# Which engine's queue issues the stores and loads of an SSD step: from SyncE to ScalarE, in a hybrid decoder block

## Chip, core and metric

One core of a Trainium2 chip runs the whole program; all data are fp32. The time is the device time of one execution in microseconds; a kernel's time is the median of several executions.

## The reference

One decoder block over 1024 tokens of 1024 channels, with two mixers side by side and a gated MLP behind them:

```python
u = rmsnorm(h)
gate_a, gate_s, b_a, c_a, v_a, z, xbc, dt_raw = split(u @ w_in)
y_a = (b_a * causal_dwconv3(c_a * v_a)) @ w_a_out
xs, bs, cs = split(silu(causal_dwconv4(xbc) + b))
y = ssd_chunked_scan(xs, softplus(dt_raw + dt_bias), a, bs, cs) + d_skip * xs
y_s = group_rmsnorm(y * silu(z)) @ w_s_out          # 4 groups of 512 channels
h = h + (sigmoid(gate_a) * y_a + sigmoid(gate_s) * y_s) @ w_o
v = rmsnorm(h)
h = h + (silu(causal_dwconv3(v @ w_1) + b) * (v @ w_3)) @ w_down
out = rmsnorm(h)
```

The SSD scan runs over 8 chunks of 128 tokens, for 4 groups of 8 heads (64 channels a head, 128 states a group). Per chunk and group it needs

```python
decay_in = exp(where(causal, a_cum[l] - a_cum[s], -inf))         # per head, 128 x 128
y_diag   = (C B^T * decay_in) @ (dt x)
y_off    = exp(a_cum) * (C @ state)
state    = exp(a_cum[-1]) * state + B^T @ (decay_to_end * dt x)
```

## The kernel before

**Projections.** A projection is done for two blocks of 128 output columns at a time (a pair). By a seven-product scheme over halves of tokens and channels a pair takes seven products, named after their operands (`a11`, `a12`, `s1`, `s2`, `s3`, `a22`, `s4`; their weights `b11`, `b21`, `t1`, `t2`, `t3`, `t4`, `b22`). Each product is 12 matmuls of 128x512 (L255), since each operand is split in a high and a low part. The weights come as two raw tiles of 512 KB a pair (`raw_1`, `raw_2`, loads L158, three buffers), GpSimd forms `t1` to `t4` from them (L292, L293, L304, L310), ScalarE casts the high part (L148, `h_`) and GpSimd or VectorE subtracts for the low one (L149, `l_`).

**SSD steps.** `xBC` goes through the convolution (taps on VectorE, L536), Silu on ScalarE, and is stored to DRAM (`ssd_in<-cv`, L545); `z` too (L561), and the tanh of the gates (L596, `gad`, `gsd`). An SSD step works on one chunk of one group; there are 32 (group by group, 8 chunks each). It loads the decay tile `m` (L630: the negated cumulative log-decay of eight heads, spread over the partitions, 512 KB, two buffers) and `in` (L633: the chunk's x, B, C; two buffers). ScalarE makes the decays (eight Relu with a bias, L639, one Exp, L640). PE transposes x and B (`px`, `pb`) and forms `pc` (L645 to L649); ScalarE copies `pb` to `bk` (L666) and scales `xe` (L658); VectorE makes `xd` (L651), `cb` and `m*cb` (L669). Loads of `eb` (exp of a_cum, two DMAs, L675) and `zt` (the chunk's z, L680, one buffer) follow. PE then does `pd`, `po` and `pst` (L687, L694, L700); VectorE adds `pd` (L702), GpSimd adds `eb` (L704), GpSimd scales the state (`st`, L711), VectorE adds `pst` to it (L715), multiplies by `zt` (L717), and `y` is stored (`yd`, L718). ScalarE squares y (L721), VectorE halves the squares (L722, L724), PE sums them over partitions (`pn`), VectorE and GpSimd make the norm factor `yr` of 128 tokens (L729, L731), and it is stored as 128 single elements (`rd`, L732). All DMAs are issued by SyncE (SP) in queue order: a store that waits for its data holds up what is queued behind it.

**Order of the work.** 8 pairs run first (`BEFORE`), then 29 (`BESIDE`), 203 products. Behind each product `tick()` counts one on, and calls what is due at that count: stage by stage, step `s` is emitted at tick `D0 + DSTEP * s` plus the offset of the stage (`STAGES`: the load of m, of in, decays, transposes, loads of eb and zt, products, squares, norm). The tile scheduler then orders the instructions of each engine by when they can start and by their place in the program, so an engine's order follows the emission only loosely. PSUM holds four buffers `mm` and four `sd`; the `sd` ones serve the products `t1`, `t4`, `b22` and all of the SSD step's, so a late reader of one (`bk` of `pb`, `st` of `pst`) holds up a product. Behind the mixer come sums of `w_down` (`wd`, `td`, many DMAs), `ya`, `so`, the output projection and the MLP; from L816 on these read `gad`, `rd` and `yd`.

Of the kernel before, what the change touches and what calls it, by code (L numbers as in the profile page):

```python
# [11 lines left out]
ALU = mybir.AluOpType  # L12
# [3 lines left out]
P = 128  # L16
# [6 lines left out]
HG = NH // NG  # L23
HD = 64
# [3 lines left out]
NCH = SEQ // P  # L28
# [21 lines left out]
)  # L50


D0, DSTEP = 12, 6
STAGES = LOAD_M, LOAD_IN, DECAY, TRANS, LOAD_Z, DIAG, SQUARES, NORM = -11, -8, -6, -4, -3, 0, 3, 6


AHEAD = 300
# [8 lines left out]
def tile_block(  # L66
# [25 lines left out]
    pe, dve, act, pool, sp = nc.tensor, nc.vector, nc.scalar, nc.gpsimd, nc.sync  # L92
# [38 lines left out]
    def tiny(name, w=1):  # L131
        return scr.tile([P, w], F32, tag="tiny", name=name, bufs=12)
# [30 lines left out]
    nhalf = const([P, 1], "nhalf")  # L163
# [167 lines left out]
    xd_ = [dram.tile([P, 10, SEQ], F32, name=f"ssd_in{g}") for g in range(NG)]  # L331
# [4 lines left out]
    acd = dram.tile([2, P, P], F32, name="acd")  # L336
    yd, rd = {}, {}
# [20 lines left out]
    for t in range(0, NCH, 2):  # L358
        xt = big_tile(f"x{t}", shape=(P, 2, DM))
# [17 lines left out]
    cdb = scm.tile([P, 4, NH, 2], F32, name="cdb")  # L377
# [51 lines left out]
    for j in range(0, 4, 2):  # L429
# [3 lines left out]
        p = Pair(U, w_in[GA + j], w_in[GA + j + 1], f"g{GA + j}", cur["row"])  # L433
        p.first(b4(f"gt{j}"), True)
        head.append(p)
    p = Pair(U, w_in[GA + 4], w_in[GA + 5], f"g{GA + 4}")
# [103 lines left out]
    def conv4(ci, t):  # L540
        cv = b4(f"cv{t}")
        taps(cv, ci, scw[:, t, :], scb[:, t : t + 1])
        act.activation(cv, cv, AF.Silu)
        g, slot = ssd_slot(t)
        sp.dma_start(xd_[g][:, slot, :], cv)  # L545

    def xbc_pair(t):
        cis = [s4(f"xbc{t + i}") for i in range(2)]
# [7 lines left out]
    def z_pair(t):  # L556
        zs = [b4(f"z{t + i}") for i in range(2)]
        pair(U, w_in[ZZ + t], w_in[ZZ + t + 1], f"z{t}", *zs)
        for i, z in enumerate(zs):
            act.activation(z, z, AF.Silu)  # L560
            sp.dma_start(xd_[(t + i) // 4][:, 6 + (t + i) % 4, :], z)  # L561


    taken = {}
# [28 lines left out]
    def gates_done(gts, dst, j):  # L593
        for i, gt in enumerate(gts):
            act.activation(gt, gt, AF.Tanh, scale=0.5)
            sp.dma_start(dst[:, j + i, :], gt)  # L596

    for i, p in enumerate(head):
        if i:
# [9 lines left out]
    def heads(t):  # L609
        return t.rearrange("p (h d) -> p h d", h=HG)  # L610

    def tiles(t):
        return t.rearrange("p (j l) -> p j l", j=4)

    states, stats = {}, {}

    def ssd_chunk(s):

        g, c = divmod(s, NCH)
        nm = f"{g}_{c}"  # L620
        q, cc = c // 2, c % 2
        hsl = slice(g * HG, (g + 1) * HG)
        ts = slice(c * P, (c + 1) * P)
        hts = slice((c % 4) * P, (c % 4 + 1) * P)

        hq = slice(q * NH + g * HG, q * NH + (g + 1) * HG)


        m = ssp.tile([P, HG, P], F32, tag="m", name=f"m{nm}", bufs=2)
        sp.dma_start(m, acd[cc, hq].unsqueeze(0).to_broadcast([P, HG, P]))  # L630
        yield
        inp = ssp.tile([P, 6, P], F32, tag="in", name=f"in{nm}", bufs=2)
        sp.dma_start(inp, xd_[g][:, 0:6, ts])  # L633
        xt, bt, ct = inp[:, 0:4, :], inp[:, 4, :], inp[:, 5, :]
# [37 lines left out]
        eb = c2(f"eb{nm}")  # L672
        if c > 0:
            for i in range(2):
                sp.dma_start(  # L675
                    tiles(eb)[i * HD : (i + 1) * HD],
                    ead[cc, hq.start + i : hq.stop : 2].unsqueeze(0).to_broadcast([HD, 4, P]),
                )
        zt = ssp.tile([P, 4, P], F32, tag="z", name=f"zt{nm}", bufs=1)
        sp.dma_start(zt, xd_[g][:, 6:10, ts])  # L680
        yield

        st = states.get(g)
        pd = sd_tile(f"pd{nm}")
        for h in range(HG):
            i, j = h % 2, h // 2
# [11 lines left out]
        if c < NCH - 1:  # L698
            pst = sd_tile(f"pst{nm}")
            pe.matmul(pst, bk, xe, start=True, stop=True)  # L700
        dve.tensor_tensor(xt, xt, tiles(pd), op=ALU.add)
        if st is not None:  # L702
            dve.tensor_tensor(eb, po, eb, op=ALU.mult)
            pool.tensor_tensor(xt, xt, tiles(eb), op=ALU.add)  # L704
        if c < NCH - 1:
            if st is None:
                st = ssp.tile([P, HALF], F32, tag="st", name=f"st{g}", bufs=1)
                act.copy(st, pst)
                states[g] = st
            else:  # L710
                pool.tensor_tensor(  # L711
                    heads(st), heads(st),
                    cdb[:, q, hsl, cc : cc + 1].to_broadcast([P, HG, HD]), op=ALU.mult,
                )
                dve.tensor_tensor(st, st, pst, op=ALU.add)  # L715

        dve.tensor_tensor(xt, xt, zt, op=ALU.mult)  # L717
        sp.dma_start(yd[g, c // 4][:, :, hts], xt)  # L718
        yield
        sq = eb  # L720
        act.activation(sq, xt.rearrange("p j l -> p (j l)"), AF.Square)  # L721
        dve.tensor_tensor(sq[:, : 2 * P], sq[:, : 2 * P], sq[:, 2 * P :], op=ALU.add)  # L722
        sums = ssp.tile([P, P], F32, tag="ss", name=f"ss{nm}", bufs=1)
        dve.tensor_tensor(sums, sq[:, :P], sq[:, P : 2 * P], op=ALU.add)  # L724
# [2 lines left out]
        pe.matmul(pn, sums, ones[:, :1], start=True, stop=True)  # L727
        rs = tiny(f"yss{nm}")
        dve.tensor_scalar(rs, pn, 1.0 / HALF, EPS, op0=ALU.mult, op1=ALU.add)  # L729
        r = tiny(f"yr{nm}")  # L730
        pool.tensor_tensor(r, rs, nhalf, op=ALU.pow)  # L731
        sp.dma_start(rd[g, c // 4][hts].unsqueeze(1), r)  # L732
        yield

    def at(n, f):
# [3 lines left out]
    for s in range(NS):  # L739
        d = D0 + DSTEP * s  # L740
        ch = ssd_chunk(s)
        for o in STAGES:
            at(d + o, lambda ch=ch: next(ch))
# [253 lines left out]
    for i in range(NFF):  # L997
# [5 lines left out]
        cv = b4(f"fcv{i}")  # L1003
# [221 lines left out]
```

## Time and profile before

| what | value |
| --- | --- |
| median of 3 runs | 2109.27 us (2107.75 to 2114.36) |
| the profiled execution's own time | 2107.57 us |
| its span in the trace | 2105.9 us |
| its mean granted clock of PE | 0.967 |
| busy in the span: PE, DVE, POOL, ACT | 1956.1, 1365.6, 1306.4, 904.3 us |
| stretch 0 to 285: PE busy, clock, DMA share | 262.00 us of 285, 0.96, 0.36 |
| stretch 285 to 1081, with 30 of the 32 SSD steps | 697.02 us of 796, 0.94, 0.58 |
| stretch 1081 to 1200 | 115.25 us of 119, 1.00, 0.92 |
| stretch 1200 to 2105 | 881.81 us of 905, 0.99, 0.47 |

Names are those of the program without buffer numbers. In a row "A <- B: 10.5, 6, 2.9" the instruction A waited for B, 10.5 us in 6 waits, the longest 2.9. A row of a timeline gives start, duration (us), engine, line, operation, `out<-in`, and in square brackets the idle time ahead and who ended it. SPq and ACTq are the sequencers of SP and ACT, which issue DMAs; PEld is PE's loading of weights. "DMA share" is the mean busy share of the 16 DMA engines.

### The profile page before, as it was taken

Reading aid. Unit: us, or ns where it says so; the run is one execution under the profiler, and the core shown is the slowest. Engines: PE = TensorE matmul, PEld = TensorE weight load, DVE = VectorE, ACT = ScalarE, POOL = GpSimd, SP = SyncE. Lnnn points to the kernel's source line nnn. Section 1 sums busy time; section 2 is a strip of 40 time slices with the busy share of each in tenths; the row PEclk is TensorE's granted clock in tenths of the full one; section 3 lists DMA queues with packets and bytes.
Section 4 is the critical chain, followed back from the end, with each engine's and each line's share of the span. In section 5 each row is a group of like instructions: output and inputs, shape, how many; then the busy total and the mean of one; then the engine's idle time right before and its main releaser. Section 6 shows DMA issues by size and latency. Waiting matters only on the chain.

```text
span 2105.9 us, 26136 instructions
## 1 busy us (share of the span) xinstructions
PE 1956.1 (93%) x8978; PEld 1594.3 (76%) x8978; DVE 1365.6 (65%) x1588; ACT 904.3 (43%) x1687; POOL 1306.4 (62%) x959
## 2 busy tenths in 40 slices
PE   6899998997998989897899999997999999999998
PEld 5788877776776777675677888886788888887887
DVE  8756986755676557664567562438776677784555
ACT  5354455444744553533333332444433333343444
POOL 7777785674666567566744432347888778853552
PEclk9899998999999999999899999998999999999999
DMA  4243235545445743667999674442322234468664
GB/s 145 72 157 105 110 131 139 147 119 137 146 119 111 158 142 97 128 165 212 249 282 389 244 248 159 159 161 97 120 105 103 98 130 155 146 210 285 198 200 150
DMA packets 184724, 338.47 MB, mean 161 GB/s; under 512 B 19856, under 2 KB 92304, under 8 KB 183568
## 3 DMA queue, kind: packets, MB, share of 16 engines
q1 hardware_dynamic: 184592, 336.80, 52.0%
q8 instruction: 71, 1.16, 0.3%
q14 instruction: 61, 0.50, 0.1%
HBM read 247.34 MB, written 89.41 MB: 160 GB/s over the span
## 4 chain that ended last, share of the span: by engine, by line
PE 41%; DMA 9%; DVE 2%; POOL 1%; issue 1%; ACT 0%; SPq 0%; POOLq 0%; ACTq 0%; DVEq 0%
PE so L255 7%; DMA td<-wd 3%; PE d L1018 3%; PE d L1020 3%; PE d L1019 3%; PE pt4up L255 3%; PE pb22up L255 3%; PE pt3up L255 3%; PE pt2up L255 3%; PE pb11up L255 3%; PE pt1up L255 3%; PE pb21up L255 3%; PE ya L255 2%; DMA wd<-in_w_down 2%; PE wo L891 1%; PE wo L892 1%
## 5 line engine op out<-in xcount | busy, mean ns | idle before, releaser
L639 ACT ACTIVATE m<-m,tk 128x128 f32<-128x128 f32 x256 | 78.8, 389 | 196.7 <-DMA m<-acd 182.6
L536 DVE SCALAR_TENSOR_TENSOR cv<-xbc,scw,cv 128x1024 f32<-128x1024 f32 x72 | 128.2, 1803 | 18.1 <-ACT cv L532 18.1
L536 DVE SCALAR_TENSOR_TENSOR fcv<-fci,fcw,fcv 128x1024 f32<-128x1024 f32 x44 | 77.8, 1768 | 27.9 <-ACT fcv L532 27.9
L149 POOL TENSOR_TENSOR l_ws<-raw_ws,h_ws 128x512 fp32r<-128x512 f32 x32 | 45.8, 1433 | 78.9 <-issue 29.0
L722 DVE TENSOR_TENSOR eb<-eb 128x256 f32<-128x256 f32 x32 | 21.3, 666 | 83.7 <-ACT eb L721 83.3
L148 ACT CAST h_ws<-raw_ws 128x512 fp32r<-128x512 f32 x64 | 38.5, 621 | 81.5 <-PE so L255 54.7
L255 PE MATMUL so<-yh,h_ws 128*128 128x512 f32 x256 | 69.6, 393 | 1.5 <-ACT h_ws L148 0.7
L658 ACT ACTIVATE xe<-px,tk 128x64 f32<-128x64 f32 x256 | 55.9, 329 | 31.0 <-DVE xd L651 30.9
L255 PE MATMUL so<-yl,h_ws 128*128 128x512 f32 x256 | 68.8, 389 | 0.0
L255 PE MATMUL so<-yh,l_ws 128*128 128x512 f32 x256 | 68.7, 390 | 0.0
L149 DVE TENSOR_TENSOR l_ws<-raw_ws,h_ws 128x512 fp32r<-128x512 f32 x32 | 29.0, 910 | 59.2 <-PE so L255 34.3
L149 POOL TENSOR_TENSOR l_wo<-raw_wo,h_wo 128x512 fp32r<-128x512 f32 x24 | 33.3, 1390 | 52.1 <-ACT h_wo L148 25.0
L292 POOL TENSOR_TENSOR t1up<-raw_2up,raw_1up 128x512 f32<-128x512 f32 x22 | 34.6, 1572 | 46.3 <-DMA raw_2up<-in_w_up 41.8
L715 DVE TENSOR_TENSOR st<-st,pst 128x512 f32<-128x512 f32 x24 | 16.5, 687 | 70.7 <-POOL st L711 63.3
L255 PEld LDWEIGHTS so<-yh,h_ws 128*128 128x128 f32 x256 | 47.4, 188 | 12.8 <-ACT h_ws L148 2.3
L717 DVE TENSOR_TENSOR in<-in,zt 128x512 f32<-128x512 f32 x32 | 44.4, 1388 | 18.7 <-POOL in L704 18.1
L255 PEld LDWEIGHTS so<-yh,l_ws 128*128 128x128 f32 x256 | 48.0, 188 | 10.5 <-DVE l_ws L149 0.5
L255 PEld LDWEIGHTS so<-yl,h_ws 128*128 128x128 f32 x256 | 48.1, 188 | 10.1
L148 ACT CAST h_wo<-raw_wo 128x512 fp32r<-128x512 f32 x48 | 29.7, 622 | 56.7 <-PE wo L892 26.8
L891 PE MATMUL wo<-l_wo,mh 128*128 128x512 f32 x128 | 50.9, 398 | 3.2 <-DVE l_wo L149 3.2
L1006 DVE TENSOR_TENSOR fcv<-fcv,h 128x1024 f32<-128x1024 f32 x22 | 38.9, 1767 | 22.6 <-ACT fcv L1005 22.6
L149 POOL TENSOR_TENSOR l_wa<-raw_wa,h_wa 128x512 fp32r<-128x512 f32 x16 | 27.8, 1743 | 39.3 <-PE ya L255 16.7
(1060 smaller groups left out, 6734.5 us busy)
## 6 DMA issues: line engine op xcount, KB each, us to landing
m<-acd SPq DMA_DIRECT2D x32, 512.0 KB, 5.6
raw_ws<-in_w_s_out SPq DMA_DIRECT2D x32, 512.0 KB, 4.2
ssd_in<-cv SPq DMA_DIRECT2D x24, 512.0 KB, 2.7
in<-ssd_in SPq DMA_DIRECT2D x32, 384.0 KB, 3.8
raw_wo<-in_w_o SPq DMA_DIRECT2D x24, 512.0 KB, 3.4
wd<-in_w_down SPq DMA_DIRECT2D x22, 512.0 KB, 6.2
td<-wd SPq DMA_DIRECT2D x44, 256.0 KB, 5.9
raw_1up<-in_w_up SPq DMA_DIRECT2D x22, 512.0 KB, 3.4
```

The lines of the kernel that those rows point to most:

```text
L148: act.copy(hi, v)
L149: (eng or pool).tensor_tensor(lo, v, f32(hi), op=ALU.subtract)
L255: pe.matmul(ps, wt[:, k, :], ct[:, k, :], start=(start and n == 0), stop=(stop and n == 11),)
L536: dve.scalar_tensor_tensor(cv, ci[:, j : j + SEQ], w[:, j : j + 1], cv, op0=ALU.mult, op1=ALU.add)
L639: act.activation(m[:, h, :], m[:, h, :], AF.Relu, bias=a)
L658: act.activation(xe[:, hc], px[:, hc], AF.Copy, scale=tk[:, 2, cc, q, g * HG + h : g * HG + h + 1],)
L717: dve.tensor_tensor(xt, xt, zt, op=ALU.mult)
L891: pe.matmul(pss[t], mh, wl, start=False, stop=False)
L1006: dve.tensor_tensor(cv, cv, h3, op=ALU.mult)
L1018: pe.matmul(ps, aa[0][:, ts], bb[0], start=k == 0, stop=False)
L1019: pe.matmul(ps, aa[0][:, ts], bb[1], start=False, stop=False)
L1020: pe.matmul(ps, aa[1][:, ts], bb[0], start=False, stop=k == KF - 1)
```

## The change

- ScalarE issues, in place of SyncE: the stores of cv, z, the gates and y, and the loads of m, eb (two) and zt. SyncE keeps the loads of weights and of `in`, and the stores of `tad` and `rd`.
- D0 goes from 12 to 11, LOAD_M from −11 to −9: all stages are emitted one tick earlier, the load of m one later, at tick 2 + 6s, where the squares of step s − 2 are emitted just ahead of it.
- The store of y stands behind the square of the same tile.
- The scaling of the state by its decay (GpSimd) is emitted ahead of the addition of `pd`.
- The norm factors of four chunks are gathered in a tile of 128x4 and stored once: 8 stores of 512 elements in place of 32 of 128.

```diff
--- before.py
+++ after.py
@@ -50,8 +50,8 @@
 )
 
 
-D0, DSTEP = 12, 6
-STAGES = LOAD_M, LOAD_IN, DECAY, TRANS, LOAD_Z, DIAG, SQUARES, NORM = -11, -8, -6, -4, -3, 0, 3, 6
+D0, DSTEP = 11, 6
+STAGES = LOAD_M, LOAD_IN, DECAY, TRANS, LOAD_Z, DIAG, SQUARES, NORM = -9, -8, -6, -4, -3, 0, 3, 6
 
 
 AHEAD = 300
@@ -542,7 +542,7 @@
         taps(cv, ci, scw[:, t, :], scb[:, t : t + 1])
         act.activation(cv, cv, AF.Silu)
         g, slot = ssd_slot(t)
-        sp.dma_start(xd_[g][:, slot, :], cv)
+        act.dma_start(xd_[g][:, slot, :], cv)
 
     def xbc_pair(t):
         cis = [s4(f"xbc{t + i}") for i in range(2)]
@@ -558,7 +558,7 @@
         pair(U, w_in[ZZ + t], w_in[ZZ + t + 1], f"z{t}", *zs)
         for i, z in enumerate(zs):
             act.activation(z, z, AF.Silu)
-            sp.dma_start(xd_[(t + i) // 4][:, 6 + (t + i) % 4, :], z)
+            act.dma_start(xd_[(t + i) // 4][:, 6 + (t + i) % 4, :], z)
 
 
     taken = {}
@@ -593,7 +593,7 @@
     def gates_done(gts, dst, j):
         for i, gt in enumerate(gts):
             act.activation(gt, gt, AF.Tanh, scale=0.5)
-            sp.dma_start(dst[:, j + i, :], gt)
+            act.dma_start(dst[:, j + i, :], gt)
 
     for i, p in enumerate(head):
         if i:
@@ -627,7 +627,7 @@
 
 
         m = ssp.tile([P, HG, P], F32, tag="m", name=f"m{nm}", bufs=2)
-        sp.dma_start(m, acd[cc, hq].unsqueeze(0).to_broadcast([P, HG, P]))
+        act.dma_start(m, acd[cc, hq].unsqueeze(0).to_broadcast([P, HG, P]))
         yield
         inp = ssp.tile([P, 6, P], F32, tag="in", name=f"in{nm}", bufs=2)
         sp.dma_start(inp, xd_[g][:, 0:6, ts])
@@ -672,12 +672,12 @@
         eb = c2(f"eb{nm}")
         if c > 0:
             for i in range(2):
-                sp.dma_start(
+                act.dma_start(
                     tiles(eb)[i * HD : (i + 1) * HD],
                     ead[cc, hq.start + i : hq.stop : 2].unsqueeze(0).to_broadcast([HD, 4, P]),
                 )
         zt = ssp.tile([P, 4, P], F32, tag="z", name=f"zt{nm}", bufs=1)
-        sp.dma_start(zt, xd_[g][:, 6:10, ts])
+        act.dma_start(zt, xd_[g][:, 6:10, ts])
         yield
 
         st = states.get(g)
@@ -698,6 +698,11 @@
         if c < NCH - 1:
             pst = sd_tile(f"pst{nm}")
             pe.matmul(pst, bk, xe, start=True, stop=True)
+        if st is not None and c < NCH - 1:
+            pool.tensor_tensor(
+                heads(st), heads(st),
+                cdb[:, q, hsl, cc : cc + 1].to_broadcast([P, HG, HD]), op=ALU.mult,
+            )
         dve.tensor_tensor(xt, xt, tiles(pd), op=ALU.add)
         if st is not None:
             dve.tensor_tensor(eb, po, eb, op=ALU.mult)
@@ -708,17 +713,13 @@
                 act.copy(st, pst)
                 states[g] = st
             else:
-                pool.tensor_tensor(
-                    heads(st), heads(st),
-                    cdb[:, q, hsl, cc : cc + 1].to_broadcast([P, HG, HD]), op=ALU.mult,
-                )
                 dve.tensor_tensor(st, st, pst, op=ALU.add)
 
         dve.tensor_tensor(xt, xt, zt, op=ALU.mult)
-        sp.dma_start(yd[g, c // 4][:, :, hts], xt)
         yield
         sq = eb
         act.activation(sq, xt.rearrange("p j l -> p (j l)"), AF.Square)
+        act.dma_start(yd[g, c // 4][:, :, hts], xt)
         dve.tensor_tensor(sq[:, : 2 * P], sq[:, : 2 * P], sq[:, 2 * P :], op=ALU.add)
         sums = ssp.tile([P, P], F32, tag="ss", name=f"ss{nm}", bufs=1)
         dve.tensor_tensor(sums, sq[:, :P], sq[:, P : 2 * P], op=ALU.add)
@@ -727,9 +728,12 @@
         pe.matmul(pn, sums, ones[:, :1], start=True, stop=True)
         rs = tiny(f"yss{nm}")
         dve.tensor_scalar(rs, pn, 1.0 / HALF, EPS, op0=ALU.mult, op1=ALU.add)
-        r = tiny(f"yr{nm}")
-        pool.tensor_tensor(r, rs, nhalf, op=ALU.pow)
-        sp.dma_start(rd[g, c // 4][hts].unsqueeze(1), r)
+        if c % 4 == 0:
+            stats[g, c // 4] = tiny(f"yr{nm}", 4)
+        r = stats[g, c // 4]
+        pool.tensor_tensor(r[:, c % 4 : c % 4 + 1], rs, nhalf, op=ALU.pow)
+        if c % 4 == 3:
+            sp.dma_start(rd[g, c // 4].rearrange("(c p) -> p c", c=4), r)
         yield
 
     def at(n, f):
```

In the changed kernel the lines behind the edit move: L702 is the state's scaling, L706 the addition of `pd`, L709 that of `eb`, L716 `st`, L718 the product with `zt`, L721 the square, L722 the store of y, L734 `yr`, L736 the store of `rd`.

How the instructions stand on three engines, before and after. First ScalarE around the decays of one step, the seventh of the second group (`m1_6`; `h_` are casts of weights, `eb1_4` the square of the step two before, `bk1_5` the copy of the transposed B); before:

```order
L148 CAST h_t4cv3_5256<-t2cv3_5181 128x512
L148 CAST h_b22cv3_5313<-raw_2cv3_5178 128x512
L639 ACTIVATE m1_6_5130<-m1_6_5130,tk_225 128x128 x5
L282 COPY m1cv3_5132<-pb11cv3_5113 128x512
L639 ACTIVATE m1_6_5130<-m1_6_5130,tk_225 128x128 x3
L148 CAST h_b21ba2_5386<-raw_1ba2_5338 128x512
L721 ACTIVATE eb1_4_4996<-in1_4_4818 128x512
L640 ACTIVATE m1_6_5130<-m1_6_5130 128x1024
L666 COPY bk1_5_5172<-pb1_5_5156 128x128
```

The same place on ScalarE in the changed kernel:

```order
L148 CAST h_t4cv3_5275<-t2cv3_5172 128x512
L630 DMA m1_6_5166<-acd_92 128x1024
L639 ACTIVATE m1_6_5166<-m1_6_5166,tk_225 128x128 x8
L148 CAST h_b22cv3_5293<-raw_2cv3_5169 128x512
L640 ACTIVATE m1_6_5166<-m1_6_5166 128x1024
L721 ACTIVATE eb1_4_4960<-in1_4_4781 128x512
L722 DMA yd11_99<-in1_4_4781 512x1x128
L680 DMA zt1_5_5164<-ssd_in1_85 128x4x128
L666 COPY bk1_5_5132<-pb1_5_5116 128x128
```

The load of m has come to stand directly ahead of the activations that read it, and ahead of the square of step s − 2, though it is emitted behind it; the store of y and the load of zt stand between the square and `bk`.

Now SyncE's queue around the first steps of the second group (`raw_` are weight loads, `rd01_96` and `yd10_97` stores of norm factors and of y); before:

```order
L158 DMA raw_2z10_4698<-in_w_in 128x1024
L732 DMA rd01_96<-yr0_7_4248 128x1
L630 DMA m1_2_4297<-acd_92 128x1024
L545 DMA ssd_in2_86<-cv9_4147 128x1024
L718 DMA yd10_97<-in1_0_3996 512x1x128
L680 DMA zt1_1_4372<-ssd_in1_85 128x4x128
L675 DMA eb1_1_4369<-ead_109 64x4x128 x2
L561 DMA ssd_in2_86<-z8_4154 128x1024
L633 DMA in1_2_4402<-ssd_in1_85 128x6x128
L158 DMA raw_1cv2_4846<-in_w_in 128x1024
```

The same place on SyncE in the changed kernel:

```order
L633 DMA in1_1_4171<-ssd_in1_85 128x6x128
L158 DMA raw_1z10_4607<-in_w_in 128x1024
L736 DMA rd01_96<-yr0_4_3604 128x4x1
L158 DMA raw_2z10_4682<-in_w_in 128x1024
L633 DMA in1_2_4362<-ssd_in1_85 128x6x128
L158 DMA raw_1cv2_4867<-in_w_in 128x1024
```

Of ten transfers the loads of weights and of `in` are left, and one store of norm factors for four chunks.

Last, GpSimd around the scaling of the state (`st1`) in the fifth step of the second group; before:

```order
L304 TENSOR_TENSOR t3ba2_5456<-raw_2ba2_5412 128x512
L731 TENSOR_TENSOR yr1_3_5068<-yss1_3_5066,nhalf_80 128x1
L711 TENSOR_TENSOR st1_4263<-st1_4263,cdb_226 128x512
L704 TENSOR_TENSOR in1_4_4818<-in1_4_4818,eb1_4_4996 128x512
L149 TENSOR_TENSOR l_b11ba2_5342<-raw_1ba2_5338,h_b11ba2_5341 128x512
```

The same place on GpSimd in the changed kernel:

```order
L734 TENSOR_TENSOR yr1_0_4415<-yss1_3_5031,nhalf_80 128x1
L304 TENSOR_TENSOR t3ba2_5473<-raw_2ba2_5395 128x512
L702 TENSOR_TENSOR st1_4234<-st1_4234,cdb_226 128x512
L709 TENSOR_TENSOR in1_4_4781<-in1_4_4781,eb1_4_4960 128x512
L149 TENSOR_TENSOR l_b11ba2_5346<-raw_1ba2_5342,h_b11ba2_5345 128x512
```

The scaling of the state stays behind `t3`, which needs the pair's second weight tile, and ahead of the addition of `eb`.

## The prediction

> **What bounds the kernel now.** I read the page first, then the busy times by stretch, then the waits of TensorE and of the others in the stretch where it idles, and last the timelines around its longest waits.
>
> ```profile
> span 2105.9 us, 26136 instructions
> ```
>
> The first number of a stretch is its length; then come the busy times of PE, PE's weight loads, DVE, ACT and POOL, the granted clock, the DMA share and GB/s.
>
> ```profile
> 285.00:1081.00 796.00, 697.02 (x3421) 556.81 (x3422) 511.18 (x651) 375.83 (x882) 506.89 (x393) 0.94 0.58 153
> ...
> 1100.00:1150.00 50.00, 47.04 (x206) 37.86 (x204) 32.86 (x40) 17.14 (x25) 21.88 (x14) 1.00 1.00 360
> 1200.00:1300.00 100.00, 100.00 (x439) 82.13 (x438) 49.74 (x58) 31.66 (x48) 29.05 (x21) 1.00 0.55 184
> ```
>
> From 1200 PE is full, and the change alters no instruction there. What can move lies in the 796 us from 285 to 1081, where 30 of the 32 SSD steps run beside the projections: PE idles 796 − 697 = 99 us there, and at a granted clock of 0.94 its work takes about 48 us (796 × 0.06) more than at full clock. No other engine is near its limit (DVE 511, POOL 507, ACT 376 of 796), nor the DMA (0.58). So it is order and lateness: which waits of PE end last?
>
> ```profile
> PE pc L649 <- DVE st L715: 10.5, 6, 2.9
> ...
> PE pt1xb L255 <- ACT bk L666: 9.8, 1, 9.8
> ...
> PE pb22ba L255 <- DVE ba L312: 6.1, 1, 6.1
> ...
> PE pt1z L255 <- ACT bk L666: 5.9, 1, 5.9
> ...
> PE pb22z L255 <- ACT bk L666: 5.2, 1, 5.2
> ...
> PE pb22cv L255 <- ACT bk L666: 4.3, 1, 4.3
> ...
> PE pt4xb L255 <- ACT bk L666: 3.6, 1, 3.6
> PE pt1cv L255 <- DVE st L715: 3.5, 2, 3.0
> PE pt1g L255 <- DVE st L715: 3.0, 1, 3.0
> PE pt1ba L255 <- DVE st L715: 2.7, 1, 2.7
> ```
>
> (Total us, times, longest.) Two families: PSUM held by `bk` on ACT (28.8 us) and by `st` on DVE (19.7 us). Behind each stands a wait of another engine:
>
> ```profile
> ACT m L639 <- DMA m<-acd: 182.6, 26, 16.4
> ...
> DVE st L715 <- POOL st L711: 63.3, 17, 8.3
> ```
>
> ACT's decay activations (L639) stand ahead of `bk` and of the casts of weights, and wait for the load of the decay tile `m`. DVE's `st` waits for POOL's. That load stands in SP's queue, among stores that wait for results:
>
> ```profile
> SPq L718 <- DVE in L717: 105.4, 27, 8.2
> ...
> SPq L732 <- POOL yr L731: 97.5, 26, 9.7
> ```
>
> One case in full: SP, then ACT, then PE.
>
> ```profile
> 832.55 0.33 SPq L732 DMA_DIRECT2D rd<-yr  x1
> 832.97 1.42 SPq L630 DMA_DIRECT2D m<-acd  x1
> ```
> ```profile
> 844.91 0.40 ACT L639 ACTIVATE m<-m,tk 128x128 f32<-128x128 f32 x1 [10.94 <-DMA m<-acd]
> ```
> ```profile
> 849.30 1.22 PE L255 MATMUL pb22ba<-us4h,h_b22ba 128*128 128x512 f32 x2 [6.06 <-DVE ba L312]
> ```
>
> The store of `r` (512 bytes in 128 writes of one element) goes out 0.42 us ahead of the load, and the load reaches ACT 11.9 us after its issue. The moved bytes from 826 to 846, in slices of 0.5 us, show why:
>
> ```profile
> GB/s 0 0 0 0 0 0 0 0 0 229 229 401 189 0 34 0 0 0 0 0 0 0 57 8 25 33 0 16 8 25 8 8 16 123 336 348 349 345 271 120
> ```
>
> For about 9 us everything slumps behind the small writes, then the 512 KB come at 340 GB/s. Where a weight load stands ahead instead:
>
> ```profile
> 883.42 0.38 SPq L630 DMA_DIRECT2D m<-acd  x1
> ```
> ```profile
> 887.62 0.99 ACT L639 ACTIVATE m<-m,tk 128x128 f32<-128x128 f32 x3 [3.59 <-DMA m<-acd]
> ```
>
> There it takes 4.2 us, and PE runs on without a gap. The first and the last pair of that kind are issued at
>
> ```profile
> 323.87 0.37 SPq L630 DMA_DIRECT2D m<-acd  x1
> ...
> 1014.52 0.48 SPq L630 DMA_DIRECT2D m<-acd  x1
> ```
>
> and I count eight in all among the 30 steps: 8.1 to 13.1 us each from issue to use, the others mostly 4.2 to 6.4.
>
> **The change part by part.** *Loads of `m`, on ACT's queue, behind the squares.* No `r` store can stand ahead of it on ACT's queue, and no store that waits on SP. The bk family (28.8) and the 6.1 (the case above) go: **−35 us**. Next late is ACT itself: the load is now issued only once ACT reaches it, directly ahead of the eight L639 that need it. What excuses this is that ACT's sequencer runs ahead of its engine:
>
> ```profile
> L721 ACTq EVENT_SEMAPHORE  x2: 17/28/38, 591.6 to 591.7; - x2
> L721 ACT ACTIVATE eb<-in x1: 630/630/630, 599.1 to 599.1; 128x512 f32<-128x512 f32 x1
> ```
>
> The sequencer dealt with the square at 591.7, the engine came to it at 599.1. So a load may go out while earlier casts still run.
>
> *SP without the stores of y, cv, z and gates.* SP keeps weight loads, `in`, `tad` and the new `r` store. Its wait for `in` of DVE (105 us) goes, most of L732's as well, so the second weight tile of a pair comes on time. That matters for `st`:
>
> ```profile
> 396.05 1.28 POOL L292 TENSOR_TENSOR t1ba<-raw_2ba,raw_1ba 128x512 f32<-128x512 f32 x1 [7.49 <-DMA raw_2ba<-in_w_in]
> ...
> 401.77 1.05 POOL L711 TENSOR_TENSOR st<-st,cdb 128x512 f32<-128x512 f32 x1
> ```
>
> POOL waited 7.5 us for a weight tile, and its scaling of `st` came 5.7 us behind. The scaling's earlier place in the source hardly moves it on POOL, so this part depends on SP alone, and I take two thirds of 19.7: **−13 us**.
>
> Idle falls by 48 of 99 us. The low clock comes with the idling (0.94 here, 1.00 where PE is full), so I let it go in proportion: 48 × 48/99 = **−23 us**. Gross −71.
>
> *Costs: ACT's issues.*
>
> ```profile
> L675 SPq DMA_DIRECT2D eb<-ead x56: 579/607/3518, 316.2 to 1057.7; - x56
> ```
> ```profile
> L680 SPq DMA_DIRECT2D zt<-ssd_in x32: 379/622/5712, 193.6 to 1048.2; - x32
> ```
> ```profile
> L718 SPq DMA_DIRECT2D yd<-in x32: 550/552/618, 304.5 to 1077.7; - x32
> ```
>
> 56 × 0.61 + 32 × 0.62 + 32 × 0.55 + 30 × 0.38 for `m` (883.42) + about 32 stores of cv, z and gates at the same 0.38 = 34 + 20 + 18 + 11 + 12 = 95 us, 3.1 us a step, on a queue that is busy 376 of 796 us. Hidden while the sequencer is ahead: 0. Unhidden everywhere: 95. I take an eighth, **+12 us**, nearer the hidden end because ACT's engine sits idle over half the stretch. The y store moved behind the square finds its data ready, as the square reads the same tile: 0; on SP it would have waited. A load of `zt` or `eb` that has to wait for its buffer now holds ACT's casts, and PE behind them; that is in the 12.
>
> *The `r` stores: 8 of 512 elements in place of 32 of 128.*
>
> ```profile
> rd<-yr SPq DMA_DIRECT2D x31, 0.5 KB, 9.1
> ```
>
> The trace has no store of 4 elements per partition. Bounds: 9 us of slump if rows go side by side, as the store of `ced` (128 pieces of 8 bytes) suggests; 36 if the count of elements decides.
>
> ```profile
> 91.28 0.38 SPq L508 DMA_DIRECT2D ced<-ce  x1
> ```
> ```profile
> GB/s 164 164 238 229 303 426 426 139 123 140 134 134 3 106 25 0 25 25 82 16 188 352 252 111 113 16 0 0 0 0 0 0 90 401 410 148 82 123 344 164
> ```
>
> (86 to 106 in slices of 0.5 us.) Behind it the rate is low for under 4 us. I take 12 us for a new one, nearest the `rd` row. 24 slumps less is in the 71 already; a slump hits all queues, `m` on ACT's too, in 8 steps of 32: 8 × 1.25 = **+10 us** (0 to 8 × 17).
>
> *Given back.* 1100 to 1150 runs at a DMA share of 1.00 with the sums of `w_down`; a PE that gets there 71 us sooner doesn't shorten those transfers. Bounds: 0 (SP is freer, they start sooner too) and 71 (they end as before). I take **+8 us**, near the low end, since PE idles only 3 us in that stretch although it is full.
>
> The stages one tick earlier (D0) and `m` one tick later: a tick is one product, 796 us over 203, 4 us; the last step ends 4 us sooner, with PE's own products still to do: 0. The later `m` has two ticks less, 8 us, ahead of its use; it is paid for in the 12 above.
>
> Sum: −35 − 13 − 23 + 12 + 10 + 8 = −41. The profiled execution took 2107.6 us (span 2105.9); 2107.6 − 41 = 2066.6. The median of the runs before is 2109.3, 1.7 above it: **2068 us**. A difference of 0.3% (6 us), the spread of the three runs, is what can be told from none.
>
> **The rivals.** *ACT becomes the late queue (slower).* A load directly ahead of its user on an in-order engine exposes its latency: issue 0.4 plus 5 us, 30 times. For it: ACT's casts feed every product of PE, and the squares now ahead wait for DVE. Against it: the sequencer's lead of 7 us above. Each microsecond per step that PE feels costs 30 × 1.48 (the clock included) = 44 us. The gain left is 71 − 18 = 53, with the other two costs off, so from 1.2 us per step on it is slower; at 2 us, 2107.6 − 53 + 89 = **2144 us**. Chance 0.10. At 0.8 us it gives 2090: 0.08.
>
> *The `r` store scales with its elements (slower).* A slump of 36 us is more than weight tiles cover. An estimate of that cover: three raw tiles, of which each feeds three or four products of 4 us, some 20 us with the split ones. 8 × (36 − 20) = 128 us of idle: 2107.6 − 71 + 20 + 128 = **2185 us**. It turns from gain to loss at a slump of 26 us (8 × 6.4 = 51). For it: one element per write is the same size as before. Against it: `ced`. Chance 0.06. The Trainium skill ("DMA: Bandwidth & Descriptors", Specifications) says that a transfer under 512 B makes the DMA engine read, modify and write; by that the same 4096 small writes would cost the same in all, which speaks for this rival; the two slumps above agree that such writes are dear, not on how they add up.
>
> *The queue doesn't matter (no change).* The transfers share one set of engines, which the slump at 835 shows to hit everything; if that, not SP's order, makes `m` late, the moves give nothing, and the eight long stores cost what 24 short ones saved: **2109 us**. Against it: 883.42, 4.2 us beside 11.9. Chance 0.10. The Trainium skill ("Trainium Kernel Development and Optimization", Key Constraints) states that transfers issued from SP, ACT and POOL run on the same 16 engines and that several issuers only save issue time. The trace shows what it leaves out: on one queue the issuer also waits for stores' data, 105 and 97 us here.
>
> *Every late step recovers.* Idle falls to 25 us (a quarter), −74, clock −36, costs +12 for ACT alone: 2107.6 − 98 = **2010 us** or less. For it: the remaining 44 us of small waits may be the same cascade. Chance 0.10.
>
> **How the numbers follow.** My forecast, 2068 with its own range of 2025 (costs at their hidden ends, 2037, and the small waits with them) to 2100 (costs doubled, 2098), has 0.56. Faster: 0.56 + 0.08 + 0.10 = 0.74; same 0.10; slower 0.10 + 0.06 = 0.16. The range for 8 in 10 leaves out the long slump (0.06), most of ACT's (0.08) and half of the big recovery (0.05): 2008 to 2115.
>
> **What would show it.** Right: ACT's wait for `m` with no single one above 8 us; PE's waits behind `bk` and `st` gone; idle from 285 to 1081 near 50 us and the clock near 0.97; SP waiting for weight buffers, not for `in` of DVE or `yr`. Wrong: eight gaps of 10 us or more in PE behind the new `r` stores; ACT's `m` wait still at 180 us with PE's casts behind it (the first rival); or an unchanged PE idle with only the names of the waits changed.

## The result and the profile after

| | before | changed |
| --- | --- | --- |
| median | 2111.08 us (2107.75 to 2114.36, 4 runs) | 2039.18 us (2035.02 to 2042.32, 4 runs) |
| ratio | | 0.9658, 95% interval 0.9633 to 0.9683 |
| profiled execution: own time, span | 2107.57, 2105.9 us | 2035.02, 2033.3 us |
| its mean granted clock | 0.967 | 0.981 |

The change makes the kernel 3.4% faster, more than the forecast of 2068 and inside its range. From one profiled execution to the other it is 72.6 us.

The stage of the SSD steps ends where PE starts on `ya`: at 1080.77 us before, at 1005.50 after. The busy times of the changed kernel from 285 us to that end, its columns as in the prediction:

```profile
285.00:1005.50 720.50, 673.40 (x3414) 540.01 (x3412) 526.76 (x646) 377.77 (x878) 512.14 (x389) 0.97 0.55 166
```

The same stretch of the kernel before, to its own end:

```profile
285.00:1080.77 795.77, 696.79 (x3420) 556.58 (x3421) 510.95 (x651) 375.83 (x882) 506.66 (x393) 0.94 0.58 153
```

The stage is 75.3 us shorter. PE's idle time in it falls from 99.0 to 47.1 us (−51.9), and the same matmuls take 23.4 us less at a clock of 0.97 in place of 0.94. Behind the stage 2.7 us are given back. The busy times of the other engines change little (the most is DVE's, 511 to 527 us).

PE's waits in the changed kernel, in that stretch (total us, times, longest):

```profile
PE pst L700 <- DVE yss L730: 13.1, 6, 3.1
PE pc L649 <- DVE st L716: 11.7, 8, 5.5
PE pt1ba L255 <- DVE st L716: 4.7, 1, 4.7
PE po L694 <- DVE gt L314: 3.0, 1, 3.0
...
PE pt4g L255 <- ACT bk L666: 1.1, 1, 1.1
...
PE pt1z L255 <- DVE st L716: 0.5, 1, 0.5
```

The family behind `bk` is gone but for 1.1 us, and so is the wait for `ba`. The family behind `st` is not: 16.9 us of 19.7 are still there. What these engines wait for:

```profile
ACT m L639 <- DMA m<-acd: 94.3, 22, 9.4
DVE st L716 <- POOL st L702: 68.7, 18, 11.6
```

ACT's wait for `m` is half of what it was (182.6), its longest 9.4 in place of 16.4. DVE's wait for GpSimd's scaling of the state has not become shorter (63.3 before). SyncE's queue in the changed kernel:

```profile
SPq L633 <- DMA yd<-in: 229.8, 27, 18.9
SPq L158 <- DVE yss L730: 53.4, 10, 9.9
...
SPq L736 <- POOL yr L734: 24.2, 7, 7.4
```

It no longer waits for results of y, cv, z and the gates, but the waiting has not gone: the load of `in` (L633) needs a buffer that is free only once the store of y has landed, and the weight loads stand behind that. This wait was there before the change too, at less than half:

```profile
SPq L633 <- DMA yd<-in: 97.6, 22, 9.3
```

### The profile page after: what moved, and what is told of

It reads as the page before. It is cut to its first block, busy times and chain, and to the rows that moved or that the text cites. A ratio compares the mean times of both kernels' runs of the same rounds, so it can differ in the third digit from the quotient of the medians.

```text
span 2033.3 us, 25995 instructions
## 1 busy us (share of the span) xinstructions
PE 1933.0 (95%) x8978; PEld 1578.5 (78%) x8978; DVE 1390.5 (68%) x1588; ACT 909.9 (45%) x1687; POOL 1309.6 (64%) x959
## 3 DMA queue, kind: packets, MB, share of 16 engines
q10 hardware_dynamic: 61696, 70.27, 11.6%
## 4 chain that ended last, share of the span: by engine, by line
PE 63%; DMA 13%; DVE 9%; POOL 7%; issue 5%; ACT 3%; SPq 0%; ACTq 0%; POOLq 0%; DVEq 0%
PE so L255 7%; PE pt2up L255 3%; PE pt4up L255 3%; DMA wd<-in_w_down 3%; PE pt3up L255 3%; PE pb22up L255 3%; PE pb11up L255 3%; PE pt1up L255 3%; PE pb21up L255 3%; PE d L1022 2%; PE d L1024 2%; PE d L1023 2%; PE ya L255 2%; PE pb22xb L255 1%; PE pt4xb L255 1%
## 5 line engine op out<-in xcount | busy, mean ns | idle before, releaser
L149 POOL TENSOR_TENSOR l_wo<-raw_wo,h_wo 128x512 fp32r<-128x512 f32 x24 | 34.3, 1432 | 50.8 <-ACT h_wo L148 24.9
L716 DVE TENSOR_TENSOR st<-st,pst 128x512 f32<-128x512 f32 x24 | 16.5, 686 | 71.0 <-POOL st L702 68.7
L718 DVE TENSOR_TENSOR in<-in,zt 128x512 f32<-128x512 f32 x32 | 44.9, 1404 | 18.8 <-POOL in L709 16.4
L669 DVE TENSOR_TENSOR m<-m,cb 128x1024 f32<-128x1024 f32 x32 | 53.2, 1662 | 0.4
L896 PE MATMUL wo<-h_wo,ml 128*128 128x512 f32 x128 | 50.8, 398 | 0.0
```

The lines of the kernel that those rows point to most:

```text
L149: (eng or pool).tensor_tensor(lo, v, f32(hi), op=ALU.subtract)
L669: dve.tensor_tensor(m, m, cb.unsqueeze(1).to_broadcast([P, HG, P]), op=ALU.mult)
L896: pe.matmul(pss[t], ml, wh, start=False, stop=k == NK - 1)
```

## The experiments

The kernel before took 2111, 2100, 2100 and 2099 us in the four sets of runs (the result and the three sets below), so kernels are compared by their ratio to the kernel before in the same set. In the table each is the kernel before or the changed kernel with the difference named; m, r, and so on are the loads and stores of these tiles.

| run | kernel | ratio | 95% interval | stage, us | PE idle in it, us | ACT's wait for m | st's for GpSimd |
| --- | --- | --- | --- | --- | --- | --- | --- |
| | before | 1 | | 795.8 | 99.0 | 182.6 | 63.3 |
| e1_gather_only | before, r gathered | 0.9725 | 0.9698 to 0.9753 | 734.7 | 58.0 | 146.8 | 46.5 |
| e2_m_on_act | before, m on ScalarE | 0.9806 | 0.9783 to 0.9828 | 750.1 | 66.0 | 119.0 | 67.0 |
| f1_gather_m_act | before, both | 0.9621 | 0.9606 to 0.9637 | 712.0 | 44.8 | 98.4 | 55.1 |
| g2_row_m_act | before, m on ScalarE, r as rows | 0.9567 | 0.9544 to 0.9591 | 698.5 | 35.0 | 68.8 | 24.9 |
| | changed | 0.9658 | 0.9633 to 0.9683 | 720.5 | 47.1 | 94.3 | 68.7 |
| g1_changed_again | changed, once more | 0.9675 | 0.9654 to 0.9696 | 724.7 | 45.9 | 99.9 | 64.7 |
| e3_no_gather | changed, r in 32 stores | 0.9857 | 0.9834 to 0.988 | 751.6 | 72.5 | 103.2 | 83.7 |
| e4_m_on_sp | changed, m on SyncE | 0.9715 | 0.9688 to 0.9742 | 728.6 | 50.6 | 126.3 | 58.7 |
| f2_row_store | changed, r as rows | 0.962 | 0.9599 to 0.9641 | 710.1 | 35.3 | 83.8 | 24.3 |
| f3_in_later | changed, in emitted later | 0.9673 | 0.9656 to 0.969 | 711.5 | 41.5 | 91.2 | 64.6 |
| f4_eb_doubled | changed, eb in 4 pieces | 0.9712 | 0.9695 to 0.9729 | 722.3 | 46.6 | 89.5 | 67.6 |
| g3_eb_zt_on_sp | changed, eb and zt on SyncE | 0.9696 | 0.9678 to 0.9713 | 726.9 | 51.7 | 110.7 | 69.6 |
| g4_stores_on_sp | changed, y, cv, z, gates on SyncE | 0.9693 | 0.9668 to 0.9719 | 720.6 | 44.7 | 97.6 | 72.7 |

The stage runs from 285 us to the first `ya` in each profiled execution; the idle time is its length less PE's busy time. The profiled executions lie anywhere in a kernel's spread of about 0.3%, so a few us between two stages tell nothing; the ratios decide.

### First four: which of the two suspects makes m late

My theory was that both count, the small writes of the norm factors and SyncE's queue. One rival had the small writes alone, the other the queue alone.

**e1_gather_only.** Edit to the kernel before:

```diff
-        r = tiny(f"yr{nm}")
-        pool.tensor_tensor(r, rs, nhalf, op=ALU.pow)
-        sp.dma_start(rd[g, c // 4][hts].unsqueeze(1), r)
+        if c % 4 == 0:
+            stats[g, c // 4] = tiny(f"yr{nm}", 4)
+        r = stats[g, c // 4]
+        pool.tensor_tensor(r[:, c % 4 : c % 4 + 1], rs, nhalf, op=ALU.pow)
+        if c % 4 == 3:
+            sp.dma_start(rd[g, c // 4].rearrange("(c p) -> p c", c=4), r)
```

> The kernel before with one edit: the norm factors of four chunks are gathered and stored once (8 stores of 512 elements on SyncE). If small writes ahead of the load of m make it late, and both the queue and their number count (my theory), most of the eight long loads go: 25 to 40 us faster, ACT's wait for m from 183 to about 130 us. If the small writes alone are the cause (rival), the whole gain is here: 60 to 75 us faster. If only SyncE's waiting stores are the cause (second rival): within 6 us of the kernel before, the eight long loads still there behind other stores.

0.9725, so 56 us (2044.1 beside 2099.9): between what my theory and the rival gave. The edit has a second effect that I had not named: 24 stores fewer stand in SyncE's queue, and SyncE's waits for `yr` fall from 97.5 to 20.5 us. So this run alone doesn't tell small writes from queue; f1_gather_m_act and g2_row_m_act do, further down. PE's longest waits of this kernel:

```profile
PE pt1xb L255 <- ACT bk L666: 10.1, 1, 10.1
PE pb22z L255 <- ACT bk L666: 9.6, 1, 9.6
```

Two of the old gaps are still there, and ACT still waits 146.8 us for `m`. Ahead of both gaps one of the eight stores that are left goes out 0.47 us before the load of `m`; the pairs are

```profile
480.58 0.37 SPq L735 DMA_DIRECT2D rd<-yr  x1
481.05 0.44 SPq L630 DMA_DIRECT2D m<-acd  x1
```
```profile
660.38 0.37 SPq L735 DMA_DIRECT2D rd<-yr  x1
660.85 0.50 SPq L630 DMA_DIRECT2D m<-acd  x1
```

and ACT gets to work on `m` at 492.60 and 674.68, 11.6 and 13.8 us after the issue. This is the case of the prediction again. For y and cv SyncE waits longer than before (105.4 and 52.7):

```profile
SPq L718 <- DVE in L717: 159.7, 27, 12.8
SPq L545 <- ACT cv L543: 63.3, 9, 12.3
```

**e2_m_on_act.** Edit to the kernel before:

```diff
-        sp.dma_start(m, acd[cc, hq].unsqueeze(0).to_broadcast([P, HG, P]))
+        act.dma_start(m, acd[cc, hq].unsqueeze(0).to_broadcast([P, HG, P]))
```

> The kernel before with one edit: the load of m is issued by ScalarE, at its old tick. My theory: it gets past SyncE's stores, but the 32 slumps behind the norm factors still hit it: 20 to 35 us faster, the waits behind bk mostly gone. Small writes alone: within 6 us. ScalarE as the late queue: slower, with ACT's wait for m at 183 us or more and PE's waits behind casts longer.

0.9806, 41 us faster, a little past what I gave. The rival in which ScalarE becomes the late queue falls: ACT's wait for `m` went down to 119.0 with the load directly on its own queue, and so did PE's waits behind `bk`:

```profile
PE pb22cv L255 <- ACT bk L666: 2.5, 1, 2.5
PE pt4xb L255 <- ACT bk L666: 1.5, 1, 1.5
```

The rival of the small writes alone (no more than 6 us) falls too.

**e3_no_gather.** Edit to the changed kernel: the lines of e1_gather_only the other way round.

> The changed kernel without the gathering: 32 stores of 128 single elements again, all else as changed. My theory: 24 more slumps of 9 us, each felt by loads on every queue: 15 to 30 us slower than the changed kernel (2054 to 2069). Small writes alone: 2095 or more. Queue alone: within 6 us of 2039.

0.9857 beside 0.9658: 42 us slower than the changed kernel, more than my theory gave (15 to 30), less than the rival's. Without the gathering the changed kernel is even slower than e2_m_on_act, in which `m` alone moved (0.9834 to 0.988 beside 0.9783 to 0.9828). So something in the other edits costs, some 11 us. As in e1_gather_only, SyncE's waits for `yr` change with the stores (24.2 to 132.4 us), so this run doesn't show the 42 us to be the small writes alone.

**e4_m_on_sp.** Edit to the changed kernel: `act.dma_start(m, ...)` back to `sp.dma_start(m, ...)`.

> The changed kernel with the load of m back on SyncE, at its new tick, all else as changed. My theory: SyncE no longer waits for y, cv, z or gates, but for the buffer of in (230 us in the changed kernel), so m comes late behind that: 10 to 25 us slower than 2039. If it is the small writes alone: within 6 us. If the issue on ScalarE costs: up to 10 us faster.

0.9715, 8 to 12 us slower than the changed kernel (0.9675 and 0.9658), at or below the low end of what I gave, and its interval overlaps with the second measurement's; a wait of 5.0 us behind `bk` is back. That this is less than the 41 us of e2_m_on_act because the stores have left SyncE is not shown: e1_gather_only, with all stores still there, is as fast (0.9725).

### Next four: what the two edits are worth together, and the costs

**f1_gather_m_act.** Edit to the kernel before: those of e1_gather_only and e2_m_on_act, and nothing else.

> The kernel before with two edits only: the gathered store of norm factors, and the load of m on ScalarE at its old tick. Theory after the first four runs (these two carry the gain, each alone 0.9725 and 0.9806 of the time before, and the stores, eb, zt, the early state and the ticks carry nothing): within 0.4% of the changed kernel's 0.966. If the moved stores carry a part of their own (rival): 0.971 or above. If the other issues on ScalarE cost what I put on them (12 us): 0.960.

0.9621. These two edits are worth the whole change, and its interval (0.9606 to 0.9637) touches the changed kernel's first one (0.9633 to 0.9683) and lies below its second (0.9654 to 0.9696). They are partly the same gain: alone they take 2.75% and 1.94%, together 3.79%. And the stores of y, cv and z are left on SyncE, with their waits:

```profile
SPq L718 <- DVE in L717: 159.7, 29, 14.0
SPq L545 <- ACT cv L543: 47.1, 7, 12.2
```

Nearly 160 us of waits for y, with weight loads behind, make this kernel no slower than the changed one, in which SyncE waits 230 us for y's landing instead. That weight loads have slack for such waits is not shown by that, since SyncE waits in both.

**f2_row_store.** Edit to the changed kernel (`ss` is a tile that is free by then):

```diff
         if c % 4 == 3:
-            sp.dma_start(rd[g, c // 4].rearrange("(c p) -> p c", c=4), r)
+            pr4 = sd_tile(f"pr4{nm}")[:4, :P]
+            pe.transpose(pr4, r, ident)
+            rt = ssp.tile([P, P], F32, tag="ss", name=f"rt{nm}", bufs=1)[:4, :]
+            act.copy(rt, pr4)
+            sp.dma_start(rd[g, c // 4].rearrange("(c p) -> c p", c=4), rt)
```

> The changed kernel, but the gathered 128x4 norm factors are transposed by TensorE, copied by ScalarE and stored as 4 rows of 512 bytes: no small writes left, 8 transposes and copies more. If the 8 long slumps of about 11 us still cost 10 us or more in all (my term): 10 to 20 us faster than the changed kernel, 0.957 to 0.961. If they lie beside other work: within 6 us of it, 0.963 to 0.969.

0.962 (0.9599 to 0.9641) beside 0.9658 and 0.9675: 8 to 12 us less, at the near end of what my term gave; the intervals overlap with the first measurement's and not with the second's. The same step from f1_gather_m_act to g2_row_m_act is clear of noise: 0.9621 to 0.9567, some 11 us, the intervals apart, and the number of stores is the same in both. In the profile, with the last small writes gone, DVE's wait for the scaling of the state falls from 68.7 to

```profile
DVE st L716 <- POOL st L702: 24.3, 12, 6.5
```

while the sum of SyncE's waits for y's landing is nearly what it was:

```profile
SPq L633 <- DMA yd<-in: 215.8, 26, 16.6
```

So the slumps had a part in the lateness of `st`. How large it is stays open, since GpSimd's order moved as well: in the fifth scaling of this stretch `st` now stands ahead of the next pair's `t1xb` (406.75 and 407.78), in the changed kernel it stands behind its `t1xb`, `t2xb` and `t3xb` (409.75 to 415.19), and there DVE waits 11.60 us.

**f3_in_later.** Edit to the changed kernel: LOAD_IN from −8 to −6.

> The changed kernel with LOAD_IN at -6 in place of -8, so that the load of in is emitted two ticks later, when the store of y that frees its buffer is nearer to its landing. If SyncE's 230 us of waits for that landing, with weight loads behind, are what holds the state (st) and PE's idle now: SyncE's wait falls below 120 us, st's wait for GpSimd by a third, 8 to 15 us faster than the changed kernel (0.959 to 0.962). If in then comes late to TensorE: px waits for in, 0.970 or more. If weight loads have slack: within 6 us of the changed kernel.

0.9673, no difference, and it tests little: SyncE's wait for y's landing stayed at

```profile
SPq L633 <- DMA yd<-in: 231.4, 28, 16.7
```

since the scheduler left the load where it was in SyncE's order, at least from 560 to 650 us. What a free SyncE would bring is not settled by this run.

**f4_eb_doubled.** Edit to the changed kernel: the load of `eb` in four DMAs of 32 partitions in place of two of 64.

```diff
             for i in range(2):
-                act.dma_start(
-                    tiles(eb)[i * HD : (i + 1) * HD],
-                    ead[cc, hq.start + i : hq.stop : 2].unsqueeze(0).to_broadcast([HD, 4, P]),
-                )
+                for o in range(0, HD, HD // 2):
+                    act.dma_start(
+                        tiles(eb)[i * HD + o : i * HD + o + HD // 2],
+                        ead[cc, hq.start + i : hq.stop : 2].unsqueeze(0).to_broadcast([HD // 2, 4, P]),
+                    )
```

> The changed kernel with each load of eb issued in four pieces of 32 partitions in place of two of 64: 56 issues more on ScalarE, the same bytes. By the term that I took (an eighth of the issue time bites): 56 x 0.6 = 34 us of issues, 4 to 5 us slower. If they are hidden: within 3 us. If ScalarE's queue is the late one: 20 us slower or more (0.975).

0.9712 (0.9695 to 0.9729), 8 to 11 us slower by the medians; the interval stands off the changed kernel's first one and overlaps with the second (0.9654 to 0.9696), and the stage was as long as in g1_changed_again (722.3 and 724.7). A small cost is likely, its size is open. It is not the 20 us of a late ScalarE.

### Last four: the remaining edits, and a better version

**g1_changed_again** is the changed kernel as it is.

> The changed kernel once more, on the chip of the three runs beside it: 0.9658 of the kernel before, within its interval (0.963 to 0.968).

0.9675: as expected, and the base for the three beside it.

**g2_row_m_act.** Edit to the kernel before: `m` on ScalarE as in e2_m_on_act, the norm factors as rows as in f2_row_store.

> The kernel before with the load of m on ScalarE and the norm factors transposed and stored as rows of 512 bytes; y, cv, z, gates, eb and zt stay on SyncE, the ticks stay. If the gathered store and the load of m carry all and the eight long slumps left cost about 8 us: 0.962 less 0.004, 0.956 to 0.960, the fastest so far. If the slumps are hidden here, where SyncE is slower anyway: 0.962.

0.9567 (0.9544 to 0.9591): the fastest, 93 us under the kernel before in its set (2006.5 beside 2099.3) and below the changed kernel by more than either interval. The waits for `m` and `st` are among the shortest of all kernels:

```profile
ACT m L639 <- DMA m<-acd: 68.8, 25, 6.0
...
DVE st L715 <- POOL st L711: 24.9, 9, 5.2
```

PE idles 35.0 us in its stage, and the clock there is 0.99:

```profile
285.00:983.49 698.49, 663.54 (x3419) 533.77 (x3419) 540.58 (x649) 375.65 (x884) 525.42 (x391) 0.99 0.54 173
```

**g3_eb_zt_on_sp.** Edit to the changed kernel: the loads of `eb` and `zt` by SyncE.

> The changed kernel with the loads of eb and zt back on SyncE (88 issues, 54 us). If ScalarE's issues bite by a fifth to a third (as the doubled eb showed, 11 us for 34 us): 8 to 16 us faster than the changed kernel, 0.958 to 0.962. If they then come late behind SyncE's waits for in's buffer: 0.970 or more, with VectorE waiting for eb. If hidden: 0.966.

0.9696, the same as 0.9675 within the intervals: 54 us of issues off ScalarE bring nothing, and being behind SyncE's waits costs nothing clear.

**g4_stores_on_sp.** Edit to the changed kernel: the stores of cv, z, gates and y by SyncE, that of y ahead of the square again.

> The changed kernel with the stores of y, cv, z and gates back on SyncE (64 issues, about 30 us); m, eb and zt stay on ScalarE. If ScalarE's issues bite and SyncE's waits for results have slack: 4 to 10 us faster than the changed kernel, 0.961 to 0.964. If SyncE's waits for results hold weight loads: 8 us slower or more, 0.970. If neither: 0.966.

0.9693, the same. The place of these stores and of these loads doesn't matter, each taken by itself.

Taken together the rest of the change does cost something. Three pairs of kernels differ in nothing but that rest (all of the change without the move of `m` and the gathering): e2_m_on_act and e3_no_gather (0.9806 and 0.9857), f1_gather_m_act and the changed kernel (0.9621; 0.9658 and 0.9675), g2_row_m_act and f2_row_store (0.9567 and 0.962). In each the kernel with the rest is slower, by 8 to 11 us, in the first and the last with the intervals apart.

## Why the prediction was right, and where its terms were not

The direction, the stage and the first mechanism were right, and the sum was 32 us short: −41 forecast, −72.6 measured between the two profiled executions. Of the signs that I had named, PE's idle time (47.1 us) and the clock (0.97) came as said and the waits behind `bk` went; those behind `st` stayed, ACT's longest wait for `m` is 9.4 us and not below 8, and SyncE waits most for the landing of y. Term by term:

| term | forecast | measured |
| --- | --- | --- |
| PE's gaps behind `bk` and `ba` | −35 | −33.8 (34.9 to 1.1) |
| PE's gaps behind `st` | −13 | −2.8 (19.7 to 16.9) |
| PE's other idle time, less the costs of ScalarE's issues and of the `r` stores | 0 + 12 + 10 | −15.3 |
| clock | −23 | −23.4 |
| behind the stage | +8 | +2.7 |
| sum | −41 | −72.6 |

The first row leaves out, as the prediction did, three small waits behind `bk` (2.9 us before); their going is in the third row.

*The first step held, cause and size.* The case that the prediction followed through three engines was the right one, and a queue on which the small stores don't stand ahead of `m` cures it: in e2_m_on_act PE's waits behind `bk`, 31.7 us in all before, are 4.0, and its idle time falls by 33 us. Fewer small stores alone (e1_gather_only) leave 25.2 us behind `bk`, 19.7 of them in the two gaps with such a store directly ahead. What the gathering shortens there is the rest: the waits behind `st` from 19.7 to 10.0, all others from 48.8 to 22.8 us (41.4 in e2_m_on_act). So the two edits take largely different waits, and why their gains still overlap (4.7% alone in sum, 3.8% together) is not settled.

*The clock term came out by luck in part.* I let the clock's part fall in proportion to the idle time, and in the changed kernel that holds. In f2_row_store the idle time falls by 63.7 us and PE's busy time by 22.0; the same rule would give 31.

*The second step failed.* I put GpSimd's late scaling of the state down to weight tiles that stand behind SyncE's stores waiting for results, and took two thirds of it away. That weight tiles stand behind a wait of SyncE holds; I had the wrong wait. The case that I had quoted, 7.5 us of GpSimd for `raw_2ba`, was this on SyncE in the kernel before:

```profile
374.72 0.39 SPq L732 DMA_DIRECT2D rd<-yr  x1
377.92 0.55 SPq L718 DMA_DIRECT2D yd<-in  x1
388.63 0.37 SPq L633 DMA_DIRECT2D in<-ssd_in  x1
390.47 0.69 SPq L158 DMA_DIRECT2D raw_2ba<-in_w_in  x1
```

SyncE waits 9.3 us there, not for a result but for the landing of y's store, which has gone out behind a small store; only then can it issue `in`, and the weight tile behind it. The change leaves this wait in place. One of PE's longest waits in the changed kernel (`pt1ba`, 4.7 us) comes the same way:

```profile
825.33 0.38 SPq L736 DMA_DIRECT2D rd<-yr  x1
825.53 0.56 ACTq L722 DMA_DIRECT2D yd<-in  x1
837.63 0.38 SPq L633 DMA_DIRECT2D in<-ssd_in  x1
839.47 0.38 SPq L158 DMA_DIRECT2D raw_1g<-in_w_in  x1
845.57 1.29 POOL L292 TENSOR_TENSOR t1g<-raw_2g,raw_1g 128x512 f32<-128x512 f32 x1 [7.80 <-DMA raw_1g<-in_w_in]
851.03 1.05 POOL L702 TENSOR_TENSOR st<-st,cdb 128x512 f32<-128x512 f32 x1
852.85 2.08 PE L255 MATMUL pt1ba<-us1h,h_t1ba 128*128 128x512 f32 x4 [4.68 <-DVE st L716]
```

SyncE waits 11.7 us for y's landing, GpSimd 7.8 for the weight tile, DVE 8.5 for the scaling that stands behind `t1g` to `t3g` in GpSimd's order, and PE 4.7 for DVE. With the small writes replaced by rows, `st`'s waits fall to 24.3 us (f2_row_store) and 24.9 (g2_row_m_act). Not all of them come from slumps: a wait of 8.99 us, for the scaling at 721.80, has no small store near it, since the one ahead went out at 650.29. There, too, the scaling stands behind the next pair's `t1` to `t3`. An edit that moves only its place on GpSimd was not run.

*The `r` stores were the right size, and in the wrong place.* Eight of them cost about what I took: 8 to 12 us by f2_row_store, 11 between f1_gather_m_act and g2_row_m_act. The one at 825.33 is shown above; the bytes moved from 825 to 845 in slices of 0.5 us:

```profile
GB/s 8 0 3 130 290 164 40 1 0 0 15 38 27 18 25 31 18 17 16 18 30 43 56 29 161 80 261 148 146 259 286 205 251 336 303 303 344 385 410 320
```

From 828 to 837 no slice is above 56 GB/s, though the store of y (825.53) waits to land all the time. From issue to landing, the eight stores took

```profile
DMA to landing us min/median/max: 8.7/10.7/14.9
```

10.7 us for four times the elements, beside 9.1 before. So the slow rival, 36 us each, falls, and the 24 slumps saved are worth far more than I counted. I had put them only into the gaps behind `m`; e3_no_gather prices the 24 stores at 42 us in the changed kernel, their waits on SyncE included. (An estimate for the slumps alone: 11 us for eight, so 33 for 24.) There PE idles 72.5 us in the stage, beside 47.1. This is where the runs put the missing gain: the slumps delay transfers other than `m` too. The store of y landed after 5.6 us (median) before, 5.4 and 5.1 in the two other kernels with 32 small stores (e2_m_on_act, e3_no_gather), 2.9 in the changed kernel (4.2 in g4_stores_on_sp, the most of any kernel with eight), and 2.7 and 2.8 with rows. So the slumps stood behind PE's many small waits as well, which I had left as they were; e1_gather_only shows these fall.

*The 12 us for ScalarE's issues are neither shown nor refuted.* Taking 54 us of issues off it, or 30 us of stores, makes no difference (g3_eb_zt_on_sp, g4_stores_on_sp). Adding 56 issues shows something, not clearly. But all of the rest of the change together costs 8 to 11 us, which is about the size of this term. Whether it is the issues together, the ticks, the place of the store of y or the earlier scaling of the state, no run tells. The rival in which ScalarE becomes the late queue falls with e2_m_on_act.

*The rule that the issuing engine doesn't matter.* The Trainium skill ("Trainium Kernel Development and Optimization", Key Constraints) says that issuing from several engines only saves issue time. For the stores, and for `eb` and `zt`, moved back one group at a time, the runs agree (g3, g4: no difference). For `m` they don't: one line moved from one queue to another, 1.9% (e2_m_on_act), and what differs is what stood ahead of it in the queue.

*What stays open.* The two edits alone reach 0.9621, the whole change 0.9658 and 0.9675. So the best kernel of the runs is not the changed one but g2_row_m_act, without the rest. Of this rest, the place of the stores and that of eb and zt are shown to matter little one by one; the ticks and the earlier scaling of the state were not tried alone. The new wait of `pst` for `yss` (13.1 us, 4.3 before) goes with the stores on ScalarE: with them back on SyncE it is

```profile
PE pst L700 <- DVE yss L730: 3.8, 4, 2.7
```

but that kernel is no faster, so this doesn't settle it.

## What to carry to other kernels

When an engine waits for a load, look at what was issued just ahead of it on the same queue and at the bytes moved in between: here 512 bytes in single elements made a load of 512 KB take 11.9 us in place of 4.2. Count such a store by all that it delays, not by the one wait in which it was found, and follow the delay on: a late landing keeps a buffer, the load that needs the buffer keeps a queue, and the queue keeps a weight tile of which the first engine knows nothing. Make the store a row of contiguous bytes if a small transpose can do that. And when a change has many parts, run the few that carry the gain without the others: here two edits do at least as well as the whole.

## What the runs showed of the hardware

- A store of a 128x1 tile to 128 single elements took 9.1 us to land, one of a 128x4 tile to 512 single elements 10.7 us (medians). The number of elements in a store mattered little. That is other than a cost per small write, which the Trainium skill's rule on transfers under 512 B ("DMA: Bandwidth & Descriptors", Specifications) suggested to me: the 4096 small writes were the same in number, in 8 stores in place of 32. The traces give no landing time for the same 512 numbers stored as 4 rows of 512 bytes; the kernel was some 11 us faster with eight of these (f1_gather_m_act to g2_row_m_act).
- While a store of single elements was under way, a 256 KB store on another engine's queue was late as well: y's, issued by ScalarE at 825.53, held SyncE until 837.63, beside a median of 2.9 us from issue to landing in that kernel.
- ScalarE's sequencer issued DMAs at 0.33 us (`m`) to 0.64 us (`zt`) each, some 98 us in a stage of 720. Taking 54 us or 30 us of these away made no difference that the runs could tell.
- The granted clock of the stage went with PE's idle time, though loosely: 0.94 at 99 us of idle, 0.96 at 66 (e2_m_on_act), 0.97 at 47; at 45 us it was 0.99 in f1_gather_m_act and 0.97 in g4_stores_on_sp, at 35 us 0.99 in g2_row_m_act and 0.98 in f2_row_store.
